# Rotary embedding on one core: batch 0 stored in four parts, a fixed order of loads and stores, tables on the ScalarE queue

## The chip, the cores and the metric

The kernel runs on one core of a Trainium2 chip. The metric is the device time of one execution in microseconds (us); the profiler's span is about 1.8 us shorter. For one core the granted TensorE clock was 1.00. Data go between HBM and the core's SBUF through 16 DMA engines; a kernel issues a transfer from a queue of one of its engines (sync = SP, ScalarE = ACT, GpSimd = POOL). What such a queue has waiting at the DMA engines is called its ring below; a transfer moves in packets, and it lands when its last completion signal comes.

## The reference

```python
def setup_inputs():
    batch, seq_len, num_heads, head_dim = (8, 2048, 16, 64)
    # x (8, 2048, 16, 64), cos and sin (2048, 32), all float32

def reference(x, cos, sin):
    x1 = x[..., :head_dim // 2]
    x2 = x[..., head_dim // 2:]
    out1 = x1 * cos - x2 * sin
    out2 = x1 * sin + x2 * cos
    return np.concatenate([out1, out2], axis=-1)    # float32
```

x is 67.1 MB and the result is 67.1 MB; each byte has to cross once.

## The kernel before

Each batch is one tile: 128 partitions, 16 rows of 1024 values in each. POOL's loads cast f32 to f16, its stores cast back. Two rows of batch 0 (the "head") and the tables come over the sync queue. VectorE rotates a batch in four operations, 26.2 us.

```python
    JA = 2
    head = const_pool.tile([P, JA, H, D], f32)
    nc.sync.dma_start(out=head..., in_=x0[:, 0:JA, :]...)
    nc.sync.dma_start(out=sin_f, in_=sin.rearrange("(p j) d -> p j d", j=J))
    nc.sync.dma_start(out=cos_f, in_=cos.rearrange("(p j) d -> p j d", j=J))

    def load(b):                       # f32 in HBM -> f16 tile, POOL queue
        xt = io_pool.tile([P, J, H, D], f16)       # NBUF = 5 of these
        j0 = JA if b == 0 else 0
        nc.gpsimd.dma_start(out=xt[:, j0:J, :, :]..., in_=x[b]...)
        return xt

    def store(b, xt):                  # f16 tile -> f32 in HBM, POOL queue
        nc.gpsimd.dma_start(out=out[b]..., in_=xt)

    def rotate(xt):
        v = tmp_pool.tile([P, J, H, D], f16)
        # ... v1 = x2 * (-sin); v2 = x1 * sin; xt = xt * cos; xt = xt + v

    tiles = [load(b) for b in range(NBUF)]
    nc.scalar.copy(out=tiles[0][:, 0:JA]..., in_=head...)
    nc.scalar.copy(out=sin_h, in_=sin_f)
    nc.scalar.mul(out=neg_h, in_=sin_f, mul=-1.0)
    nc.scalar.copy(out=cos_h, in_=cos_f)
    for b in range(B):
        rotate(tiles[b])
        store(b, tiles[b])
        if b + NBUF < B:
            tiles.append(load(b + NBUF))
    # (cut: imports, shapes, launch)
```

Of the kernel before, what the change touches and what calls it, by code (L numbers as in the profile page):

```python
# [1 line left out]

# [4 lines left out]


@with_exitstack  # L10
def kernel(
    ctx: ExitStack,
    tc: tile.TileContext,
    x: bass.AP,
    cos: bass.AP,
    sin: bass.AP,
    out: bass.AP,
):
    nc = tc.nc
    f16 = mybir.dt.float16  # L20
    f32 = mybir.dt.float32

    B, S, H, D = x.shape
    Dh = D // 2
    P = nc.NUM_PARTITIONS
    J = S // P
    NBUF = 5

    const_pool = ctx.enter_context(tc.tile_pool(name="rope_const", bufs=1))
    io_pool = ctx.enter_context(tc.tile_pool(name="rope_io", bufs=NBUF))  # L30
    tmp_pool = ctx.enter_context(tc.tile_pool(name="rope_tmp", bufs=1))

    JA = 2
    head = const_pool.tile([P, JA, H, D], f32)
    x0 = x[0].rearrange("(p j) h d -> p j (h d)", j=J)
    nc.sync.dma_start(  # L36
        out=head.rearrange("p j h d -> p (j h d)"),
        in_=x0[:, 0:JA, :].rearrange("p j f -> p (j f)"),
    )
    sin_f = const_pool.tile([P, J, Dh], f32)  # L40
    cos_f = const_pool.tile([P, J, Dh], f32)
    cos_h = const_pool.tile([P, J, Dh], f16)
    sin_h = const_pool.tile([P, J, Dh], f16)
    neg_h = const_pool.tile([P, J, Dh], f16)
    nc.sync.dma_start(out=sin_f, in_=sin.rearrange("(p j) d -> p j d", j=J))  # L45
    nc.sync.dma_start(out=cos_f, in_=cos.rearrange("(p j) d -> p j d", j=J))

    def load(b):
        xt = io_pool.tile([P, J, H, D], f16)
        j0 = JA if b == 0 else 0  # L50
        nc.gpsimd.dma_start(  # L51
            out=xt[:, j0:J, :, :].rearrange("p j h d -> p (j h d)"),
            in_=x[b].rearrange("(p j) h d -> p j (h d)", j=J)[:, j0:J, :].rearrange("p j f -> p (j f)"),
        )
        return xt

    def store(b, xt):
        nc.gpsimd.dma_start(  # L58
            out=out[b].rearrange("(p j) h d -> p (j h d)", j=J), in_=xt
        )  # L60

    def rotate(xt):
        v = tmp_pool.tile([P, J, H, D], f16)
        sin_b = sin_h.unsqueeze(2).to_broadcast([P, J, H, Dh])
        neg_b = neg_h.unsqueeze(2).to_broadcast([P, J, H, Dh])
        cos_b = cos_h.unsqueeze(2).to_broadcast([P, J, 2 * H, Dh])
        nc.vector.tensor_mul(out=v[:, :, :, 0:Dh], in0=xt[:, :, :, Dh:D], in1=neg_b)  # L67
        nc.vector.tensor_mul(out=v[:, :, :, Dh:D], in0=xt[:, :, :, 0:Dh], in1=sin_b)  # L68
        xw = xt.rearrange("p j h (e d) -> p j (h e) d", d=Dh)
        nc.vector.tensor_mul(out=xw, in0=xw, in1=cos_b)  # L70
        xa = xt.rearrange("p j h d -> p (j h d)")
        nc.vector.tensor_add(out=xa, in0=xa, in1=v.rearrange("p j h d -> p (j h d)"))  # L72

    tiles = [load(b) for b in range(NBUF)]
    nc.scalar.copy(  # L75
        out=tiles[0][:, 0:JA, :, :].rearrange("p j h d -> p (j h d)"),
        in_=head.rearrange("p j h d -> p (j h d)"),
    )
    nc.scalar.copy(out=sin_h, in_=sin_f)  # L79
    nc.scalar.mul(out=neg_h, in_=sin_f, mul=-1.0)  # L80
    nc.scalar.copy(out=cos_h, in_=cos_f)  # L81
    for b in range(B):
        rotate(tiles[b])
        store(b, tiles[b])
        if b + NBUF < B:
            tiles.append(load(b + NBUF))


# [1 line left out]
_INS = ['x', 'cos', 'sin']  # L90
_OUTS = [((8, 2048, 16, 64), 'float32')]


# [23 lines left out]
```

## Time and profile before

| | before |
|---|---|
| time, first three runs | 318.24 us (317.87 to 318.32) |
| span of the profiled run | 316.1 us |
| VectorE busy | 209.2 us (66%) |
| HBM bytes over the span | 134.7 MB, 426 GB/s |

From the page of before: the span, the busy times, the DMA engines' busy share in 40 equal slices (9 means 90% or more), the queues with their share of the 16 engines' time, and the HBM traffic.

```profile
span 316.1 us, 121 instructions
DVE 209.2 (66%) x32; ACT 4.9 (2%) x5; POOL 8.8 (3%) x20
...
DMA  9899999999999999999999999999999999999996
...
q0 software_dynamic: 2304, 100.14, 98.5%
q1 hardware_dynamic: 432, 1.57, 1.4%
HBM read 67.63 MB, written 67.11 MB: 426 GB/s over the span
```

The DMA engines hardly pause. VectorE is idle a third of the time. The waits of before (engine and line, what it waited for: us in total, times, longest) seem to offer a lot to gain:

```profile
POOL out_dram L58 <- DVE xt L72: 136.3, 4, 50.5
POOL xt L51 <- DMA out_dram<-xt: 118.3, 3, 56.4
DVE v L67 <- DMA xt<-in_x_dram: 52.0, 3, 24.8
ACT cos_h L81 <- DMA cos_f<-in_cos_dram: 17.7, 1, 17.7
```

Lines of before's timeline (start, us, engine, line, operation; what ended the idle time in brackets):

```profile
23.65 4.43 DVE L67 TENSOR_TENSOR v<-xt,neg_h 128x8192 f16<-128x8192 f16 x1 [23.65 <-DMA xt<-in_x_dram]
...
33.51 0.62 ACT L81 CAST cos_h<-cos_f 128x512 f16<-128x512 f32 x1 [17.74 <-DMA cos_f<-in_cos_dram]
...
52.14 0.54 POOL L58 DMA_DIRECT2D out_dram<-xt  x1 [48.10 <-DVE xt L72]
...
263.88 0.53 POOL L58 DMA_DIRECT2D out_dram<-xt  x1 [50.50 <-DVE xt L72]
```

The first store is issued at 52.14 us and the last at 263.88 us. The single packets in the trace tell when they really moved. For each transfer of POOL's queue, this is the start of its first packet (read from the packet records; L is a load, S a store, the digit the batch):

```
before  L0 5.16   L1 22.82  L2 42.24  L3 61.56  L4 80.89  S0 101.07 S1 120.39 L5 139.70
        L6 159.03 S2 178.35 S3 197.67 L7 216.98 S4 236.30 S5 255.62 S6 274.93 S7 294.25  last packet ends 314.28
```

A whole batch takes 19.31 to 19.33 us in the queue, load or store, whatever precedes it, but for two steps: L1 (19.42) and L4, the last load ahead of the first store (20.18). S0, issued at 52, moves at 101; S7, issued at 263.88, moves at 294.25. The queue always holds work.

### The profile page before, as it was taken

To read this page: it belongs to the slowest core of one execution; us is meant where nothing else is said; L and a number is where in the kernel's file an instruction comes from. 1 tells how busy PE (TensorE), PEld (TensorE's weight loads), DVE (VectorE), ACT (ScalarE), POOL (GpSimd) and SP (SyncE) were. 2 spreads that over 40 slices of the span, in tenths; PEclk is the share of its full clock that TensorE was granted. 3 is DMA by queue.
4 is the path that set the end of the run, shared out by engine and by line. 5 is a ranking of instruction groups with operands and counts; after the bars stand their busy time and mean duration, and the time that the engine had idled before them with its cause. 6 is when DMAs were issued, how large, how long until landed. Compare 5 with 4: busy or idle time off the path is not lost.

```text
span 316.1 us, 121 instructions
## 1 busy us (share of the span) xinstructions
DVE 209.2 (66%) x32; ACT 4.9 (2%) x5; POOL 8.8 (3%) x20
## 2 busy tenths in 40 slices
DVE  0009799999999999999879999990009993000000
ACT  4100000000000000000000000000000000000000
POOL 3000000000000000010000000100000000000000
DMA  9899999999999999999999999999999999999996
GB/s 277 182 261 208 199 236 228 199 199 265 199 199 265 398 506 423 398 336 261 199 199 224 373 398 398 506 423 265 203 328 398 398 448 481 398 398 506 423 398 265
DMA packets 2736, 101.71 MB, mean 322 GB/s; under 512 B 304, under 2 KB 304, under 8 KB 560
## 3 DMA queue, kind: packets, MB, share of 16 engines
q0 software_dynamic: 2304, 100.14, 98.5%
q1 hardware_dynamic: 432, 1.57, 1.4%
HBM read 67.63 MB, written 67.11 MB: 426 GB/s over the span
## 4 chain that ended last, share of the span: by engine, by line
issue 44%; DVE 14%; another core or an unknown queue 14%; DMA 10%; POOL 1%; SPq 0%; ACT 0%; POOLq 0%
DMA cos_f<-in_cos_dram 10%; DVE xt L70 6%; DVE xt L72 6%; DVE v L67 1%; DVE v L68 1%; POOL out_dram L58 1%; POOL xt L51 0%; ACT cos_h L81 0%; POOLq L112 0%; SPq L45 0%; SPq L36 0%; POOLq L58 0%
## 5 line engine op out<-in xcount | busy, mean ns | idle before, releaser
L70 DVE TENSOR_TENSOR xt<-xt,cos_h 128x16384 f16<-128x16384 f16 x8 | 69.5, 8692 | 2.0 <-ACT cos_h L81 1.7
L67 DVE TENSOR_TENSOR v<-xt,neg_h 128x8192 f16<-128x8192 f16 x8 | 35.4, 4426 | 52.2 <-DMA xt<-in_x_dram 52.0
L72 DVE TENSOR_TENSOR xt<-xt,v 128x16384 f16<-128x16384 f16 x8 | 69.5, 8692 | 0.3
L68 DVE TENSOR_TENSOR v<-xt,sin_h 128x8192 f16<-128x8192 f16 x8 | 35.4, 4419 | 0.0
L58 POOL DMA_DIRECT2D out_dram<-xt x8 | 4.3, 535 | 136.3 <-DVE xt L72 136.3
L51 POOL DMA_DIRECT2D xt<-in_x_dram x8 | 4.4, 559 | 119.1 <-DMA out_dram<-xt 118.3
L75 ACT CAST xt<-head 128x2048 f16<-128x2048 f32 x1 | 1.9, 1897 | 3.5 <-DMA head<-in_x_dram 3.5
L75 ACT ACT_TABLE_LOAD x1 | 1.3, 1283 | 0.7 <-PEq L101 0.7
L81 ACT CAST cos_h<-cos_f 128x512 f16<-128x512 f32 x1 | 0.6, 617 | 17.7 <-DMA cos_f<-in_cos_dram 17.7
L79 ACT CAST sin_h<-sin_f 128x512 f16<-128x512 f32 x1 | 0.6, 618 | 7.2 <-DMA sin_f<-in_sin_dram 7.2
L80 ACT ACTIVATE neg_h<-sin_f 128x512 f16<-128x512 f32 x1 | 0.6, 624 | 0.0
L101 POOL MEMSET const-float32-0.0<- 128x1 f32 x1 | 0.1, 98 | 0.2 <-issue 0.2
L101 POOL MEMSET const-bfloat16-1.0<- 128x1 bf16 x1 | 0.1, 101 | 0.0
L101 POOL MEMSET const-float32-1.0<- 128x1 f32 x1 | 0.1, 98 | 0.0
L101 POOL MEMSET const-uint8-127<- 128x1 uint8 x1 | 0.1, 98 | 0.0
## 6 DMA issues: line engine op xcount, KB each, us to landing
xt<-in_x_dram POOLq DMA_DIRECT2D x7, 4096.0 KB, 41.2
xt<-in_x_dram POOLq DMA_DIRECT2D x1, 3584.0 KB, 22.3
head<-in_x_dram SPq DMA_DIRECT2D x1, 1024.0 KB, 4.8
sin_f<-in_sin_dram SPq DMA_DIRECT2D x1, 256.0 KB, 13.4
cos_f<-in_cos_dram SPq DMA_DIRECT2D x1, 256.0 KB, 31.8
out_dram<-xt POOLq DMA_DIRECT2D x8, 66.0
```

What stands on the lines that cost most here:

```text
L51: nc.gpsimd.dma_start(out=xt[:, j0:J, :, :].rearrange("p j h d -> p (j h d)"), in_=x[b].rearrange("(p j) h d -> p j (h d)", j=J)[:, j0:J, ...
L58: nc.gpsimd.dma_start(out=out[b].rearrange("(p j) h d -> p (j h d)", j=J), in_=xt)
L67: nc.vector.tensor_mul(out=v[:, :, :, 0:Dh], in0=xt[:, :, :, Dh:D], in1=neg_b)
L68: nc.vector.tensor_mul(out=v[:, :, :, Dh:D], in0=xt[:, :, :, 0:Dh], in1=sin_b)
L70: nc.vector.tensor_mul(out=xw, in0=xw, in1=cos_b)
L72: nc.vector.tensor_add(out=xa, in0=xa, in1=v.rearrange("p j h d -> p (j h d)"))
L75: nc.scalar.copy(out=tiles[0][:, 0:JA, :, :].rearrange("p j h d -> p (j h d)"), in_=head.rearrange("p j h d -> p (j h d)"),)
L79: nc.scalar.copy(out=sin_h, in_=sin_f)
L80: nc.scalar.mul(out=neg_h, in_=sin_f, mul=-1.0)
L81: nc.scalar.copy(out=cos_h, in_=cos_f)
L101: nc = _bacc.Bacc("TRN2", target_bir_lowering=False, num_devices=1)
```

## The change

The intent: get VectorE and the stores going early, so that loads and stores run side by side and no tail of stores is left. Batch 0 is cut into rows 0-2, 2-6, 6-10 and 10-16, each stored once it is rotated (the first through ScalarE as f32 on the sync queue); the order of the POOL queue is fixed by added dependencies, and loads run three batches ahead instead of five; the tables come in over the ScalarE queue.

```diff
-    nc.sync.dma_start(out=sin_f, ...)
-    nc.sync.dma_start(out=cos_f, ...)
+    cuts = [JA, 6, 10, J]
+    nc.scalar.dma_start(out=sin_f, ...)
+    nc.scalar.dma_start(out=cos_f, ...)
+    last = []
+    def ring(dma):                     # keeps POOL's DMAs in program order
+        if last:
+            tc.add_manual_dep(dma.ins, last[-1].ins.name,
+                mybir.DependencyInfo(mybir.DependencyClass.NoSync, ...), reason="order of the ring")
+        last.append(dma)
     # ... load(b, j0, j1), store(b, j0, j1), rotate(b, j0, j1) on rows j0 to j1; load and store call ring()
-    tiles = [load(b) for b in range(NBUF)]
+    for j0, j1 in zip(cuts, cuts[1:]):
+        load(0, j0, j1)
     # ... the four ScalarE casts, as before
+    rotate(0, 0, JA)
+    nc.scalar.copy(out=flat(head), in_=flat(tiles[0][:, 0:JA, :, :]))
+    nc.sync.dma_start(out=rows(out, 0, 0, JA), in_=flat(head))
+    rotate(0, 2, 6);   store(0, 2, 6)
+    rotate(0, 6, 10);  store(0, 6, 10)
+    load(1, 0, J)
+    rotate(0, 10, 16); store(0, 10, 16)
+    load(2, 0, J); load(3, 0, J)
-    for b in range(B):
-        rotate(tiles[b]); store(b, tiles[b])
-        if b + NBUF < B: tiles.append(load(b + NBUF))
+    for b in range(1, B):
+        rotate(b, 0, J); store(b, 0, J)
+        if b + 3 < B: load(b + 3, 0, J)
     # (shortened: fresh(b), which allocates a tile, and cuts[...] written as numbers)
```

More of the change, by code (lines that the diff above doesn't have):

```diff
@@ L33 @@
     JA = 2
-    head = const_pool.tile([P, JA, H, D], f32)
-    x0 = x[0].rearrange("(p j) h d -> p j (h d)", j=J)
-    nc.sync.dma_start(
-        out=head.rearrange("p j h d -> p (j h d)"),
-        in_=x0[:, 0:JA, :].rearrange("p j f -> p (j f)"),
-    )
+    cuts = [JA, 6, 10, J]
     sin_f = const_pool.tile([P, J, Dh], f32)
@@ L44 @@
     neg_h = const_pool.tile([P, J, Dh], f16)
-    nc.sync.dma_start(out=sin_f, in_=sin.rearrange("(p j) d -> p j d", j=J))
-    nc.sync.dma_start(out=cos_f, in_=cos.rearrange("(p j) d -> p j d", j=J))
-    def load(b):
-        xt = io_pool.tile([P, J, H, D], f16)
-        j0 = JA if b == 0 else 0
-        nc.gpsimd.dma_start(
-            out=xt[:, j0:J, :, :].rearrange("p j h d -> p (j h d)"),
-            in_=x[b].rearrange("(p j) h d -> p j (h d)", j=J)[:, j0:J, :].rearrange("p j f -> p (j f)"),
-        )
-        return xt
@@ L57, in store @@
-    def store(b, xt):
-        nc.gpsimd.dma_start(
-            out=out[b].rearrange("(p j) h d -> p (j h d)", j=J), in_=xt
-        )
-    def rotate(xt):
-        v = tmp_pool.tile([P, J, H, D], f16)
-        sin_b = sin_h.unsqueeze(2).to_broadcast([P, J, H, Dh])
-        neg_b = neg_h.unsqueeze(2).to_broadcast([P, J, H, Dh])
-        cos_b = cos_h.unsqueeze(2).to_broadcast([P, J, 2 * H, Dh])
-        nc.vector.tensor_mul(out=v[:, :, :, 0:Dh], in0=xt[:, :, :, Dh:D], in1=neg_b)
-        nc.vector.tensor_mul(out=v[:, :, :, Dh:D], in0=xt[:, :, :, 0:Dh], in1=sin_b)
-        xw = xt.rearrange("p j h (e d) -> p j (h e) d", d=Dh)
-        nc.vector.tensor_mul(out=xw, in0=xw, in1=cos_b)
-        xa = xt.rearrange("p j h d -> p (j h d)")
-        nc.vector.tensor_add(out=xa, in0=xa, in1=v.rearrange("p j h d -> p (j h d)"))
@@ L74, with flat, rows @@
-    tiles = [load(b) for b in range(NBUF)]
-    nc.scalar.copy(
-        out=tiles[0][:, 0:JA, :, :].rearrange("p j h d -> p (j h d)"),
-        in_=head.rearrange("p j h d -> p (j h d)"),
-    )
+    head = const_pool.tile([P, JA, H, D], f32)
+    def flat(t):
+        return t.rearrange("p j h d -> p (j h d)")
+    def rows(t, b, j0, j1):
+        return t[b].rearrange("(p j) h d -> p j (h d)", j=J)[:, j0:j1, :].rearrange("p j f -> p (j f)")
+    nc.sync.dma_start(out=flat(head), in_=rows(x, 0, 0, JA))
@@ new lines, with load @@
+    nc.scalar.dma_start(out=sin_f, in_=sin.rearrange("(p j) d -> p j d", j=J))
+    nc.scalar.dma_start(out=cos_f, in_=cos.rearrange("(p j) d -> p j d", j=J))
+    last = []
+    def ring(dma):
+        if last:
+            tc.add_manual_dep(
+                dma.ins,
+                last[-1].ins.name,
+                mybir.DependencyInfo(mybir.DependencyClass.NoSync, mybir.DependencyReason.DATA),
+                reason="order of the ring",
+            )
+        last.append(dma)
+    def load(b, j0, j1):
+        ring(nc.gpsimd.dma_start(out=flat(tiles[b][:, j0:j1, :, :]), in_=rows(x, b, j0, j1)))
@@ new lines, in store, with rotate @@
+    def store(b, j0, j1):
+        ring(nc.gpsimd.dma_start(out=rows(out, b, j0, j1), in_=flat(tiles[b][:, j0:j1, :, :])))
+    def rotate(b, j0, j1):
+        xt = tiles[b]
+        n = j1 - j0
+        js = slice(j0, j1)
+        vt = tmp_pool.tile([P, J, H, D], f16)
+        v = vt[:, 0:n, :, :]
+        sin_b = sin_h[:, js, :].unsqueeze(2).to_broadcast([P, n, H, Dh])
+        neg_b = neg_h[:, js, :].unsqueeze(2).to_broadcast([P, n, H, Dh])
+        cos_b = cos_h[:, js, :].unsqueeze(2).to_broadcast([P, n, 2 * H, Dh])
+        nc.vector.tensor_mul(out=v[:, :, :, 0:Dh], in0=xt[:, js, :, Dh:D], in1=neg_b)
+        nc.vector.tensor_mul(out=v[:, :, :, Dh:D], in0=xt[:, js, :, 0:Dh], in1=sin_b)
+        xw = xt[:, js, :, :].rearrange("p j h (e d) -> p j (h e) d", d=Dh)
+        nc.vector.tensor_mul(out=xw, in0=xw, in1=cos_b)
+        xa = flat(xt[:, js, :, :])
+        nc.vector.tensor_add(out=xa, in0=xa, in1=flat(v))
@@ L79, with fresh @@
+    tiles = {}
+    def fresh(b):
+        xt = io_pool.tile([P, J, H, D], f16)
+        tiles[b] = xt
+    fresh(0)
+    for j0, j1 in zip(cuts, cuts[1:]):
+        load(0, j0, j1)
+    nc.scalar.copy(out=flat(tiles[0][:, 0:JA, :, :]), in_=flat(head))
     nc.scalar.copy(out=sin_h, in_=sin_f)
@@ L81 @@
     nc.scalar.copy(out=cos_h, in_=cos_f)
-    for b in range(B):
-        rotate(tiles[b])
-        store(b, tiles[b])
-        if b + NBUF < B:
-            tiles.append(load(b + NBUF))
+    rotate(0, 0, JA)
+    nc.scalar.copy(out=flat(head), in_=flat(tiles[0][:, 0:JA, :, :]))
+    nc.sync.dma_start(out=rows(out, 0, 0, JA), in_=flat(head))
+    rotate(0, cuts[0], cuts[1])
+    store(0, cuts[0], cuts[1])
+    rotate(0, cuts[1], cuts[2])
+    store(0, cuts[1], cuts[2])
+    fresh(1)
+    load(1, 0, J)
+    rotate(0, cuts[2], cuts[3])
+    store(0, cuts[2], cuts[3])
+    fresh(2)
+    load(2, 0, J)
+    fresh(3)
+    load(3, 0, J)
+    for b in range(1, B):
+        rotate(b, 0, J)
+        store(b, 0, J)
+        if b + 3 < B:
+            fresh(b + 3)
+            load(b + 3, 0, J)
 _INS = ['x', 'cos', 'sin']
```

## The prediction

> **What bounds the kernel now.** The DMA engines, nearly without a pause. The page gives HBM 67.63 MB read and 67.11 MB written in 316.1 us: 426 GB/s. DMA busy tenths are 9 or 8 in every slice from the second to the 39th. The windows view shows 431 GB/s in stores alone (102 to 121 us). In the packet records each engine starts a packet of 64 KB of f32 every 2.413 us, loads and stores alike: 16 x 65.5 KB / 2.413 us = 435 GB/s, the figure that the Trainium skill, "DMA: Bandwidth & Descriptors", section "Where 436 GB/s comes from", gives as the fabric ceiling; the trace agrees. VectorE is busy 209 us (66%); its 52 us of waits for loads and POOL's 136 and 118 us (the waits view) cost nothing: whenever POOL waits, transfers are queued. The last store, issued at 263.88, finds 30 us of queue ahead (packets from 294.25 to 314.27).
>
> The span divides so: to 1.74 us nothing moves; to 5.16 the head and some tables; to 314.27 POOL's packets; 1.8 us to the end. The third stretch, 309.1 us, holds 8 x 2.11 + 120 x 2.413 = 306.4 us of packets per engine. Only 2.7 us are anything else: table packets (about 1 us), one stall of 0.9 us where the first store follows the fifth load.
>
> **What the change does.** Bytes stay 134.7 MB. Stores begin at about 20 us rather than 52, and loads and stores alternate. In the trace a load after a store (120.39 to 139.70) takes the same 19.3 us as one after a load, so alternation gains no rate; early stores only exchange places with loads. The same page, "Issuing engines are not separate DMA queues", says all issuers share the 16 engines: the ScalarE queue adds no bandwidth. It gets the tables in earlier: now cos lands at 33.5 us because its 2 KB packets take turns with packets of 2.1 to 2.4 us. After, they run beside the head, and the rest takes turns with 16 KB packets (0.6 us, an estimate from 2.413): sin at 5 to 7 us, cos at 7 to 12. Batch 0's VectorE work (26.2 us) is cut into 3.3, 6.6, 6.6, 9.8 us; first part done at 13 to 16 us; first POOL store issued at 20 to 23, while load 0's last part and the head's store occupy the engines to about 25. The second store and load 1 follow at 27 to 30, as the first store runs out (about 30): the one place where the engines may run dry, for 0 to 2 us. From then on, adding 19.3 us per transfer and 26.2 per rotation, each store is issued 10 to 35 us before its turn.
>
> **Sum.** Gain: tables out of the way (0.5 to 1 us). Cost: a possible gap (0 to 2 us), more completions and smaller packets (about 0.3). Earlier VectorE work is not on the path. Net about 0.
>
> Predicted 317.8 us, 316.3 to 319.8 in 8 of 10. Faster by over 2%: 0.02; within 2%: 0.95; slower by over 2%: 0.03.
>
> **What would show it.** DMA busy 9 in all slices, about 426 GB/s over the span; VectorE's first instruction before 12 us, first POOL store near 21, yet span 315 to 317. Load 1 issued at 27 to 30: a dip there or none.
>
> **What would make it wrong.** A gap near 30 us longer than 2 us; a lower rate for 16 KB packets; a higher rate if reads and writes overlapped in one ring; POOL's fixed order delaying a load until the queue is empty.

## The result, and the profile after

Ratios here and below are the mean time of one kernel's fast runs over that of the other's fast runs of the same rounds, so not quite the ratio of the medians quoted.

| | before | after |
|---|---|---|
| time, median of 6 runs | 318.28 us (317.87 to 318.67) | 318.76 us (318.42 to 319.39) |
| ratio, 95% interval | | 1.0019 (1.0005 to 1.0034) |
| span of the profiled run | 316.1 us | 317.0 us |
| last DMA packet ends | 314.28 us | 314.68 us |
| last landing to the end | 1.43 us | 1.92 us |

The time is the same within 2%; a loss of about half a microsecond is just resolved. The page after, the lines that answer to those shown of before:

```profile
span 317.0 us, 145 instructions
DVE 210.8 (67%) x44; ACT 6.7 (2%) x6; POOL 11.1 (3%) x24
...
DMA  7999999999999999999999999999999999999996
...
q0 software_dynamic: 2880, 99.09, 97.8%
q1 hardware_dynamic: 288, 2.10, 1.8%
q10 hardware_dynamic: 288, 0.52, 0.5%
HBM read 67.63 MB, written 67.11 MB: 425 GB/s over the span
```

The engines were full before and are full after (q10 is the ScalarE queue with the tables). The timeline after shows that the change did all that it meant to:

```profile
10.19 0.69 DVE L79 TENSOR_TENSOR vt<-xt,neg_h 128x1024 f16<-128x1024 f16 x1 [10.19 <-ACT xt L95]
...
12.65 0.62 ACT L98 CAST cos_h<-cos_f 128x512 f16<-128x512 f32 x1 [2.49 <-DMA cos_f<-in_cos_dram]
...
23.12 0.54 POOL L68 DMA_DIRECT2D out_dram<-xt  x1 [20.14 <-DVE xt L84]
...
30.17 0.54 POOL L68 DMA_DIRECT2D out_dram<-xt  x1 [6.50 <-DVE xt L84]
30.69 0.54 POOL L65 DMA_DIRECT2D xt<-in_x_dram  x1
...
283.65 0.53 POOL L68 DMA_DIRECT2D out_dram<-xt  x1 [38.13 <-DVE xt L84]
```

VectorE starts 13 us earlier, cos is there 21 us earlier, POOL's first store is issued 29 us earlier. Yet the last store is issued at 283.65 us, 20 us *later* than before. The packet records say why (a, b, c are the parts of batch 0; the head's store, on the sync queue, moves from 21.39 us on):

```
after   L0 5.39   S0a 26.53 S0b 31.43 L1 36.29  S0c 55.58 L2 62.84  L3 82.17  S1 101.49 L4 120.81 S2 140.13
        L5 159.44 S3 178.77 L6 198.08 S4 217.41 L7 236.72 S5 256.04 S6 275.36 S7 294.68  last packet ends 314.68
```

Stores moved forward in the queue, so loads moved back. S0 begins at 26.5 us instead of 101.1; L4 begins at 120.8 instead of 80.9. The sum did not change, and S7 has its turn at 294.68 instead of 294.25. Before, it was issued 30 us ahead of that turn; now 11 us.

### The profile page after: what moved, and what is told of

The parts are those of the page before. It is cut to its first block, busy times and chain, and to the rows that moved or that the text cites. A ratio compares the mean times of both kernels' runs of the same rounds, so it can differ in the third digit from the quotient of the medians.

```text
span 317.0 us, 145 instructions
## 1 busy us (share of the span) xinstructions
DVE 210.8 (67%) x44; ACT 6.7 (2%) x6; POOL 11.1 (3%) x24
## 5 line engine op out<-in xcount | busy, mean ns | idle before, releaser
L79 DVE TENSOR_TENSOR vt<-xt,neg_h 128x8192 f16<-128x8192 f16 (+3 forms) x11 | 35.9, 3261 | 70.0 <-DMA xt<-in_x_dram 59.7
L82 DVE TENSOR_TENSOR xt<-xt,cos_h 128x16384 f16<-128x16384 f16 (+3 forms) x11 | 70.0, 6364 | 2.2 <-ACT cos_h L98 1.8
L84 DVE TENSOR_TENSOR xt<-xt,vt 128x16384 f16<-128x16384 f16 (+3 forms) x11 | 70.0, 6365 | 0.4
L80 DVE TENSOR_TENSOR vt<-xt,sin_h 128x8192 f16<-128x8192 f16 (+3 forms) x11 | 35.8, 3253 | 0.0
L68 POOL DMA_DIRECT2D out_dram<-xt x10 | 5.4, 538 | 272.1 <-DVE xt L84 272.1
L65 POOL DMA_DIRECT2D xt<-in_x_dram x10 | 5.5, 558 | 0.8 <-PEq L145 0.8
L100 ACT CAST head<-xt 128x2048 f32<-128x2048 f16 x1 | 1.9, 1898 | 2.6 <-DVE xt L84 2.6
```

The source lines that it names most:

```text
L65: ring(nc.gpsimd.dma_start(out=flat(tiles[b][:, j0:j1, :, :]), in_=rows(x, b, j0, j1)))
L68: ring(nc.gpsimd.dma_start(out=rows(out, b, j0, j1), in_=flat(tiles[b][:, j0:j1, :, :])))
L79: nc.vector.tensor_mul(out=v[:, :, :, 0:Dh], in0=xt[:, js, :, Dh:D], in1=neg_b)
L80: nc.vector.tensor_mul(out=v[:, :, :, Dh:D], in0=xt[:, js, :, 0:Dh], in1=sin_b)
L82: nc.vector.tensor_mul(out=xw, in0=xw, in1=cos_b)
L84: nc.vector.tensor_add(out=xa, in0=xa, in1=flat(v))
```

## The experiments

Theory A: the 16 DMA engines are saturated from 2 to 314 us; only bytes, dead time at the ends and pauses of the engines count. Rival B: the start of VectorE's chain is on the path, and the change's gain was given back elsewhere. Rival C: reads and writes could overlap, given the right order or queue. Rival D: POOL's fixed order makes loads wait. Theories E and F are about the last half microsecond. Each run is compared with the kernel before, run on the same chip.

### Tables alone on the ScalarE queue

```diff
-    nc.sync.dma_start(out=sin_f, ...)
-    nc.sync.dma_start(out=cos_f, ...)
+    nc.scalar.dma_start(out=sin_f, ...)
+    nc.scalar.dma_start(out=cos_f, ...)
```

> Before, with one part of the change alone: the two table loads are issued on the ScalarE queue, nothing else. Theory A (the 16 DMA engines are saturated from 2 us to 314 us, only bytes and dead time count): 317.3 to 318.4 us, ratio 0.997 to 1.000 against before; the tables' packets mostly move before POOL's first packet at 5.2 us, so sin lands at 6 to 8 us instead of 14.6, cos near 20 us instead of 33.5, and VectorE's first product with cos starts more than 8 us earlier, with no such gain in time. Rival B (the start of the VectorE chain is on the path, and the full change gives its gain back elsewhere): faster by several us, below 315.

Measured: 318.10 us against 317.82, ratio 1.0007 (0.9995 to 1.0020). No gain, and a time within the stated range. The milestones were missed, as this run's timeline shows:

```profile
10.67 0.62 ACT L79 CAST sin_h<-sin_f 128x512 f16<-128x512 f32 x1 [7.73 <-DMA sin_f<-in_sin_dram]
...
28.84 0.62 ACT L81 CAST cos_h<-cos_f 128x512 f16<-128x512 f32 x1 [15.23 <-DMA cos_f<-in_cos_dram]
32.82 8.69 DVE L70 TENSOR_TENSOR xt<-xt,cos_h 128x16384 f16<-128x16384 f16 x1
```

The first product with cos starts 1.3 us earlier than in before (34.16), not more than 8. So VectorE's chain moved hardly at all, and this run says little against B; the runs with less and with more VectorE work settle that. What it shows is that cos 4.7 us sooner is worth nothing here: the 0.5 to 1 us that the prediction booked for "tables out of the way" is not there.

### Order alone

```diff
+    # ring() as in the change, called by load and store
-    tiles = [load(b) for b in range(NBUF)]
+    tiles = [load(b) for b in range(3)]
...
-        if b + NBUF < B:
-            tiles.append(load(b + NBUF))
+        if b + 3 < B:
+            tiles.append(load(b + 3))
```

> Before, with a second part alone: three whole loads first, then store b and load b+3 in fixed alternation; batch 0 not split, tables where they were. A: same within 0.3% (317.3 to 319.2 us), each transfer of 8.4 MB of f32 takes 19.3 us whatever stands before it in the ring, no slice of DMA below 9 after the first. Rival C (alternating loads and stores lets the engines read and write at once): below 312 us and steps below 19.0 us. Rival D (POOL's fixed order makes loads wait, and that is what cancels a gain of the split): above 320 us with a visible pause of the engines.

Measured: 317.99 against 317.82, ratio 1.0004 (0.9992 to 1.0017). From the first store on, the steps from transfer to transfer stay at 19.31 to 19.33 us with loads and stores in full alternation, and the engines do not pause. C falls for one ring, and so does D.

### The full change with the tables on the sync queue

```diff
-    nc.scalar.dma_start(out=sin_f, ...)      # both lines, in the kernel after
+    nc.sync.dma_start(out=sin_f, ...)
```

> The full change with the tables back on the sync queue, behind the head. A: within 0.3% of after (317.8 to 319.5 us); cos lands at 12 to 17 us, the first part's store and the later ones shift by a few us at most, and the engines stay busy because load 0's parts, then the head's store, cover it. B: above 320 us, since the whole VectorE chain starts later.

Measured: 320.16 against 317.82, ratio 1.0069 (1.0055 to 1.0083). This missed A's range by 0.7 us and lies just above the 320 that B had named, and the timeline and windows of this run say why. In the windows: stretch, its length, busy time of VectorE, ScalarE and POOL, clock, DMA share, GB/s.

```profile
14.83 0.62 ACT L98 CAST cos_h<-cos_f 128x512 f16<-128x512 f32 x1 [4.43 <-DMA cos_f<-in_cos_dram]
...
32.35 0.54 POOL L68 DMA_DIRECT2D out_dram<-xt  x1 [6.50 <-DVE xt L84]
32.88 0.54 POOL L65 DMA_DIRECT2D xt<-in_x_dram  x1
```

```profile
31.70:33.40 1.70, 1.67 (x2) 0.00 (x0) 1.05 (x2) 1.00 0.00 0
```

cos is ready 2.2 us later than in the kernel after, so the second store (32.35 instead of 30.17) and load 1 behind it are issued 2.2 us later. The first store had run out, and all 16 engines stood still from 31.73 to 33.45. In the kernel after, the second store's first packet moved at 31.43, as the first store's last packets ended (31.43 to 32.04): no gap, but nothing to spare. So A's account stands, that only bytes and pauses count, and what I expected from it was wrong: I had assumed that the covering work would last, and it lasts just long enough for the tables' faster way. In this one stretch B is right: in the split kernel the start of VectorE's chain sets when the second store is issued. That is so for this kernel alone; for the kernel before, B is tested below. A table load worth nothing in the kernel before is worth about 1.6 us in this one (1.0069 against 1.0019), because the split had used up the cover.

### The full change without the fixed order

```diff
-        if last:
+        if False:
```

> The full change without the added dependencies that fix the ring's order: the instruction order differs in one place alone, load 1 is now issued ahead of the first two stores of batch 0. A: same as after within 0.3% (318 to 319.3 us); the pause of up to 1 us near 25 us, if there was one, is covered by load 1, so at most 0.5 us faster than after. D: 2 us or more faster than after.

Measured: 318.22 against 317.82, ratio 1.0015 (1.0002 to 1.0027). Not distinguishable from the kernel after (1.0019). In order, only load 1 differs: it comes ahead of the first two stores and covers the tight place. Where nothing pauses, there is nothing to win.

### Nearly no VectorE work

```diff
-        v = tmp_pool.tile([P, J, H, D], f16)
+        v = tmp_pool.tile([P, 1, H, D], f16)
+        xt = xt[:, 0:1, :, :]                # and the three tables cut to one row
```

> Before with nearly all VectorE work taken away (each batch rotates one of its 16 rows per partition; a wrong result on purpose); every load and store stays. Theory A (saturated DMA engines): VectorE's busy time falls from 209 us to about 15 us, stores are issued as soon as loads land, and the time stays at 317.3 to 318.6 us. Rival B (VectorE, or when it starts, is on the path): 312 us or less.

Measured: 317.92 against 317.98, ratio 0.9999 (0.9984 to 1.0013). Its page:

```profile
DVE 17.3 (5%) x32; ACT 4.9 (2%) x5; POOL 8.8 (3%) x20
...
DMA  9899999999999999999999999999999999999996
```

192 us of VectorE work went away and the time did not move. B falls for the kernel before: not one microsecond of the rotation is on its path.

### One load less

```diff
+        if b == B - 1:
+            store(b, tiles[b - 1])
+            break
         rotate(tiles[b])
         store(b, tiles[b])
-        if b + NBUF < B:
+        if b + NBUF < B - 1:
             tiles.append(load(b + NBUF))
```

> Before without the load and the rotation of the last batch; its store writes the seventh batch's result (wrong on purpose). A: 19.3 us less, as one load of 8.4 MB of f32 takes 19.3 us in the ring: 298.0 to 299.5 us, with VectorE at 183 us. If the limit were not the ring's packets but the HBM or the chain of rotations, the saving would differ clearly: under 12 us.

Measured: 298.68 against 317.98, 19.3 us less, ratio 0.9396 (0.9382 to 0.9410). The queue's price for a batch, 19.32 us, comes off whole.

### Loads and stores in different rings

```diff
-        nc.gpsimd.dma_start(out=out[b]..., in_=xt)
+        for j0 in (0, J // 2):
+            of = out_pool.tile([P, J // 2, H, D], f32)
+            nc.scalar.copy(out=of..., in_=xt[:, j0:j0 + J // 2, :, :]...)
+            nc.sync.dma_start(out=out[b]...[:, j0:j0 + J // 2, :]..., in_=of...)
     # (cut: NBUF = 3 instead of 5, and out_pool with two buffers)
```

> Loads stay on POOL's queue; ScalarE turns the result to f32 and the stores go out on the sync queue, so loads and stores stand in different rings of each engine (three input tiles, two half-batch output tiles; right result). A (an engine moves one packet at a time at 27 GB/s, whichever ring and direction): no gain, 317 to 335 us, the excess from the last rotations, since only two half batches of stores can be queued; in a stretch where both rings are full, bytes read plus written per us stay at 430 to 436 GB/s. Rival C (reads and writes overlap if they stand in different rings): under 300 us and over 480 GB/s in such a stretch.

Measured: 323.45 against 317.98, ratio 1.0184 (1.0160 to 1.0208; too near 2% to be called the same or slower), inside A's range and far from C's. From 62 to 320 us all stores and the last five loads move, 67.1 + 5 x 8.39 = 109.1 MB in HBM, which is 423 GB/s (worked out from these sizes). The 430 to 436 that I expected was for stretches in which both rings are full, and there it held: from 98 to 106 us the packet records give 245 GB/s of loads (each packet counted at its 64 KB of f32) and 188 of stores, 433 together. The mean is lower because the rate drops three times for 6 to 9 us, near 73, 153 and 233 us, as the queued stores ran out and the next load began; these drops come to about 5.5 us of transfer, which is the excess. Why they are as deep as they are was not pursued. Taking turns between the two rings neither gains nor visibly costs, and C falls here too. The Trainium skill, "DMA: Bandwidth & Descriptors", section "Issuing engines are not separate DMA queues", says that transfers run on the same 16 DMA engines and interleave, whichever engine started them; the run agrees.

### A transfer that touches no HBM

```diff
-    NBUF = 5
+    NBUF = 4
...
+    src = const_pool.tile([P, 8192], f16)
+    dst = const_pool.tile([P, 8192], f16)
+    nc.vector.memset(src, 0.0)
     tiles = [load(b) for b in range(NBUF)]
+    nc.gpsimd.dma_start(out=dst, in_=src)
```

> Before with four tiles and one more DMA that touches no HBM: 16 KB per partition (2 MB) of f16 from SBUF to SBUF, queued behind the fourth load. If each engine's own rate is the limit (A): its 16 KB packets follow each other every 0.60 us per engine as the HBM packets do (16 KB parts of load 0 in the full change: 0.61), 4.8 us in all, and the time is 322.3 to 323.8 us. If HBM is the limit: packets follow clearly faster, under 0.5 us, and less than 4 us is added.

Measured: 323.09 against 317.98, 5.1 us more, ratio 1.0164 (1.0149 to 1.0179). In the packet records the 16 KB packets of this copy follow each other every 0.607 us per engine once it runs; the 16 KB parts of the second store in the kernel after, every 0.605 us. From the copy's first packet to that of the next store it took 5.05 us (81.78 to 86.83), so the missing fifth tile cost nothing. Taking HBM out changed nothing: HBM is not the limit, and the pace of the engines' packets is, 16 KB / 0.605 us x 16 engines = 433 GB/s. Whether that pace is set in the engines or on their way to SBUF, this run does not tell. The same skill page, section "Where 436 GB/s comes from", states a fabric ceiling of 435 GB/s and says that the HBM side (about 358 GB/s) binds transfers between HBM and SBUF. The first is the rate seen here, in loads and stores on the f32 side (their f16 side in SBUF moves half the bytes); the second is not seen, with one core running.

### The same extra VectorE work in both kernels

```diff
+        for _ in range(2 if last_one else 0):      # last rotation only
+            # the two products into v once more: 4 x 4.42 us, result unchanged
```

In the kernel before:

> Before, with 17.7 us of VectorE work added to the last rotation (its two products into the temporary tile are computed three times; right result). Theory A: the last store is then issued near 281.6 us instead of 263.9, still ahead of its turn at 294.3, so the time stays at 317.5 to 318.6 us. Rival B (VectorE's chain is on the path): 330 us or more.

Measured: 318.12 against 318.12, ratio 1.0000 (0.9985 to 1.0014). The last store in its timeline:

```profile
281.43 0.53 POOL L58 DMA_DIRECT2D out_dram<-xt  x1 [67.84 <-DVE xt L75]
```

It is 17.6 us later than in before, and still 13 us ahead of its turn (294.57). B, which asked for 330 us or more, falls again for this kernel.

In the kernel after:

> The full change with the same 17.7 us added to the last rotation. In its trace the last store is issued at 283.7 us with its turn at 294.7, 11 us of slack against 30 in before. A: the store is issued near 301.4 us, its first packet moves about 1.3 us later (the delay seen at the second store, 30.17 to 31.43), so 302.6 instead of 294.7: 7 to 9 us slower than after, 325.5 to 328 us, with a pause of all engines of about 8 us before it. If the change had gained slack: under 320 us.

Measured: 325.11 against 318.12, ratio 1.0224 (1.0211 to 1.0237). The last store in its timeline, and the windows around it:

```profile
300.81 0.53 POOL L68 DMA_DIRECT2D out_dram<-xt  x1 [55.46 <-DVE xt L88]
```

```profile
287.00:295.00 8.00, 7.97 (x2) 0.00 (x0) 0.00 (x0) 1.00 0.92 393
295.00:301.90 6.90, 5.51 (x1) 0.00 (x0) 0.53 (x1) 1.00 0.00 0
```

The engines stand still for 6.4 us (295.50 to 301.91), and that is what the run takes longer than the kernel after (325.11 to 318.76, of different rounds). I had expected 7 to 9: the store was issued 0.6 us sooner, its first packet came 1.10 us after the issue, not 1.3, and the end was 0.33 us shorter (see the next section). The sign was right and it matters: the change *spent* slack, 17.7 us of VectorE work that cost nothing before cost 6 to 7 us after.

### Twelve and fifteen tiny VectorE instructions more

The kernel after ended 0.9 us later in the profile: 0.41 us until the last landing, 0.49 us between the last landing and the end. At its end each engine has a record called DRAIN. That of VectorE stood out: at 316.59, 0.22 us after the next latest of the other engines' (316.37). In before VectorE's came at 315.61, not the last one.

```diff
+    pad = const_pool.tile([P, 32], f16)
+    nc.vector.memset(pad, 0.0)
+    for _ in range(11):                 # 14 in the second run
+        nc.vector.tensor_add(out=pad, in0=pad, in1=pad)
```

> Before with twelve tiny VectorE instructions added at the start (on a tile of 32 columns, where VectorE waits anyway), the number that the split adds; DMAs untouched. Theory E (the 0.6 us that the full change costs is not in its transfers but in the program's end: after the last landing VectorE's closing drain came at 316.59 in after, 0.4 us behind the other engines, and at 315.61 in before, with them, and it goes with the length of VectorE's instruction stream): 0.3 to 0.6 us slower than before, about 318.3 us, with the late drain in the trace. If E is wrong: ratio 1.000, and the cost lies in the transfers' number.

Measured: 317.97 against 318.12, ratio 1.0004 (0.9991 to 1.0018); drain in place, 1.42 us from the last landing to the end. Theory E, as put, fell: twelve more were not enough. But the count of VectorE's recorded instructions was 62 here and 65 in the kernel after, and the records of instruction fetches showed one 0.3 us after the end of the kernel after, one 1.2 us after the end of this run, and none in before. So the place, not the number, came into question.

> As the run with twelve tiny VectorE instructions, with fifteen: VectorE's stream then has 65 recorded instructions as in the full change (before 50, the run with twelve 62, the full change with a longer last rotation 69). In all three kernels with 65 the last drain of VectorE came 0.4 us late and the stretch from the last landing to the end was 1.91 us; with 44 to 62 it was 1.2 to 1.5 us, with 69 it was 1.59. Theory F (a certain place in VectorE's stream, a boundary of what is fetched at once, costs about 0.4 us when it falls into the closing sequence, and the transfers have no part in it): last landing as in before (314.6 to 315.0), then 1.9 us, drain late, 318.2 to 318.8 us, ratio 1.001 to 1.002. If F is wrong: 1.4 us after the last landing, ratio 1.000; the late drain would then belong to something else in the change, such as its semaphores.

Measured: 318.95 against 318.39, ratio 1.0012 (1.0000 to 1.0025). VectorE's drain came 0.22 us after the others' (317.45 and 317.23), as in the kernel after, and from the last landing to the end it took 1.75 us instead of 1.42. So the late drain comes with VectorE's instruction count alone, no transfer changed; all four profiled kernels with 65 have it. The size fell short of the 1.91 expected, because the drain is worth 0.33 us and not the whole 0.49. The other 0.16 us lies ahead of it: from the last landing to the next record on GpSimd it took 0.90 us in the kernel after and in the three variants made from it, and 0.74 in before and in both runs here. What in the change causes that was not tested. The last landing of the profiled run (316.06) also lay later than stated: one engine had come 1.2 us behind the others at the stall described at the end. The time interval just touches 1.0, so of the half microsecond the drain is shown to explain about 0.3 us by the trace; the timed difference alone would not settle it. With 69 recorded instructions (the longer rotation in the kernel after) the drain came in line again and the end took 1.59 us, which is 1.92 less 0.33. That it is the fetch of instructions is inferred: the fetch's record there lies at 282.73, in the midst of VectorE's work, which shows no gap. The Trainium skill, "Runtime: NRT & Kernel Launch", section "Instruction fetch mechanics", calls the cost of crossing a block boundary "mostly hidden"; if such a crossing is what is seen here, the closing sequence is an exception.

## Why the prediction was right, point by point

- **What bounds the kernel.** Right, and now shown from four sides: no VectorE work, no change; one load less, 19.3 us less; 2 MB more without HBM, 5.1 us more; another order or another ring, no gain.
- **"Early stores only exchange places with loads."** Right: S0 went from 101 to 27 us, L4 from 81 to 121, S7 stayed at 294 to 295.
- **Milestones.** VectorE's first instruction at 10.2 us (under 12), first POOL store issued at 23.1 (20 to 23), load 1 at 30.7 (27 to 30), cos cast at 12.65 (landing 7 to 12): right but for less than a microsecond each. "Each store is issued 10 to 35 us before its turn" was too narrow: S4, issued at 167.71, had its turn 50 us later, and only the last one came down to 11.
- **The one place where the engines may run dry.** Found where it was put, at 31 us. It was 0 in the kernel after and 1.7 us with the tables 2.2 us later. The prediction said the ScalarE queue adds no bandwidth, which holds; it didn't see that this queue's head start is what closes the gap.
- **Term mis-sized: "tables out of the way (0.5 to 1 us)".** It measured nothing (ratio 1.0007, interval from -0.05% to +0.2%), with the tables moved in the kernel before by 4 to 5 us. The tables' packets take their engine time wherever they stand.
- **Term missing: the end.** The stretch after the last landing grew by 0.49 us, more than half of the growth of the span: 0.33 us with the late drain, which the longer VectorE stream brings, and 0.16 us ahead of it, of unknown cause. The rest, 0.41 us until the last landing, is near the "about 0.3 us" booked for more completions and smaller packets, but was not isolated: it is also as large as the spread between runs of one kernel.

So 317.8 was predicted and 318.76 measured: the missing gain and the missing end are about as large as the difference. The forecast had a small gain (318.24 to 317.8) where there was a small loss; the range held because what bounds the kernel was right, not because these small terms were.

No version with a right result beats the kernel before. What is left of its span beyond packets is 1.74 us at the start, 1.8 us at the end and under 3 us between.

## What to carry to other kernels

When the DMA engines are busy in every slice and bytes / time stands at the rate of the longest transfers, starting something sooner only reorders the queue; ask of each wait whether the queue held work during it. Compare the moment a transfer is issued with the moment its first packet moves: the difference is the slack, and a change that moves no time may still spend it, as 30 us became 11 here. And in a tight schedule a part that is worthless alone can be what keeps another part from costing: test the parts both alone and taken out of the whole.

## What the Trainium skill lacked or had wrong

- "DMA: Bandwidth & Descriptors", "Where 436 GB/s comes from", says that the HBM side (about 358 GB/s) binds transfers between HBM and SBUF. Read alone, this misleads for one core: with one core running, stores alone ran at 431 GB/s and an SBUF to SBUF copy took its 16 KB packets at the same pace (0.607 against 0.605 us). Elsewhere the same page ties the 358 to both cores of a pair streaming, which no run here did.
- The same page, "Specifications", gives a first-byte latency of about 1 us for POOL's DMAs and 0.6 us for those of the sync queue. POOL's agreed in mid-run with empty engines (1.10 us, twice), but its first DMA of the program, issued at 1.25 us, moved at 5.1 to 5.4 us in all runs, while the engines already had the head to move. The sync queue's first took 1.0 us (0.74 to 1.74), and its store beside a full POOL ring 3.3 to 3.6 us (17.80 to 21.39 in the kernel after).
- No page that I found has this: the last load ahead of the first transfer that reads SBUF is held up once on all engines, by about 0.9 us (step 20.2 instead of 19.3 us; at 98 us in before, at 59 us where the first store came sooner, and at 79 us ahead of the SBUF to SBUF copy). In the run with one load less it looked different: about 1.3 us, spread over the three loads ahead of the first store. The cause stays open.
- "Runtime: NRT & Kernel Launch", "Instruction fetch mechanics", calls the boundary's cost mostly hidden. With VectorE's stream at a certain length the end was 0.33 us longer (1.75 us after the last landing instead of 1.42, transfers unchanged), and a fetch is recorded 0.3 us after the end. That the boundary causes it is inferred, not shown.
